# A decoder block in fp32 on one core: the short convolution's taps, moves, gating and high and low parts spread over steps of their own

## The chip, the core and the metric

The kernel runs on one core of a Trainium2 chip. The metric is the device time of one execution in microseconds. A core has five engines that work at the same time, each through its own instructions in order: TensorE (PE in the profile; its weight loads are PEld), VectorE (DVE), ScalarE (ACT), GpSimd (POOL) and SyncE (SP, which here only starts transfers). The program orders the instructions of TensorE, VectorE, ScalarE and GpSimd itself.

## The reference, cut to what matters

```python
hn = rmsnorm(x, g_mix)
proj = hn @ w_in                        # (512, 1024) x (1024, 14344)
xa, ba, ca, za, q, k, v, o, zb, ig, fg, ga, gb = split(proj)
u = ca * xa
y = up[0:s]*w[0] + up[1:s+1]*w[1] + up[2:s+2]*w[2] + b     # up: u with two zero rows in front
ya = (ba * y * silu(za)) @ w_a_out
yb = (...mLSTM over q, k, v with the gates i, f, o, zb...) @ w_b_out
merged = sigmoid(ga) * ya + sigmoid(gb) * yb
x = x + merged @ w_o
x = x + sigmoid(rmsnorm(x, g_ple) @ w_ple_gate) * (p @ w_ple)
out = rmsnorm(x, g_final)
```

All is float32; there are 512 positions and 1024 features.

## The kernel before, in words

**Products.** Every fp32 operand is cut into a high part (rounded to fp32r) and a low part (the rest), and a product is made of three matmuls: high x high, low x high, high x low (`mm3`, L234 to L236). The large products go through one level of Strassen's scheme: seven products of half the size in place of eight (`strassen`). Each of the seven is done in two halves (i = 0, 1) of 12 matmuls, so such a block has 14 half-products.

**Steps.** Behind each half-product the program calls `step`, which runs `tick`. A tick writes out, in this order: the first piece of the work that the half-product before handed over (`fresh`); one half of the next weight's cut (`split_half`: the high part `whi` on ScalarE, L181, the low part `wlo` on VectorE, L182, and where the scheme needs sums of weights an add on VectorE, L186, or accumulating DMAs from GpSimd's queue, L157); then one piece of every generator in `active`. Each `yield` in a generator ends its piece. So a yield moves what follows to the next half-product's place in the order of all four engines. The weight for the next product is cut while the present one runs, from one of four raw tiles (`wraw`); `whi` and `wlo` have two buffers for each half. In a conv block the raw tile of the first product is used again for the third, fifth and seventh, after the accumulating DMAs have added other weights to it.

**The convolution.** It goes over four blocks of 256 channels, c = 0, 2, 4, 6 (L1084 and L1085). `sink_conv` says what happens to the results of a block. `sink(0, t, src)` gets ca and xa for 128 positions t and puts their product u into a part of `m`; for t = 2 and 3 ScalarE first copies one factor from PSUM to a temporary `cx` (tag `e`, two buffers). `sink(1, ...)` makes ba * silu(za) from `zb` (L468 to L471) and, in all blocks but the last, turns it in 32x32 blocks (L474). `after()` then finishes the block during the next block's half-products (for c = 6, during the first product with `w_a_out`): TensorE turns u (`turned`, L403, eight transposes into `ptu`), ScalarE applies the tap of the current position with the bias (L426), VectorE adds the two earlier taps (`taps`, L409), ScalarE moves the 16 pieces of the turned gate into place (L445), VectorE multiplies by the gate (L412), ScalarE takes the high part into `ya` (L413) and VectorE the low part (`rest`, L416). In the last block the gate is turned on TensorE too, and there are no moves.

**Around it.** The convolution's buffer `m` first holds the output of head 3, which leaves for DRAM (`yt_d`) while the first block runs. Behind the convolution come the products with `w_a_out`, whose left operand is `ya`, then those with `w_b_out`, `w_o` and `w_ple_gate`.

Of the kernel before, what the change touches and what calls it, by code (L numbers as in the profile page):

```python
# [11 lines left out]
AF = mybir.ActivationFunctionType  # L12
ALU = mybir.AluOpType

P = 128
S = 512
NT = S // P
# [19 lines left out]
def hybrid_block(ctx, tc, x, p, g_mix, w_in, conv_w, conv_b, w_a_out, b_gates, g_head,  # L37
                 w_b_out, w_o, g_ple, w_ple_gate, w_ple, g_final, out):
    nc = tc.nc
    act, dve, pool, pe = nc.scalar, nc.vector, nc.gpsimd, nc.tensor  # L40
# [29 lines left out]
    H2 = S // 2  # L70
# [71 lines left out]
    raws, splits, pieces, active, fresh = {}, {}, deque(), [], []  # L142
# [60 lines left out]
    def next_operand(follow=True):  # L203

        i = state["use"]
        state["use"] += 1
        while pieces:
            split_half(*pieces.popleft())
        if follow:
            queue_split()  # L210
        got = splits.pop(i)
        return [[got[kt // HH][u][:, kt % HH, :] for kt in range(HC)] for u in range(2)]
# [71 lines left out]
    def temp(tag, name=None, dt=F32):  # L284

        return tp.tile([P, S], dt, name=name or tag, tag=tag, bufs={"c": 3}.get(tag, 2))
# [3 lines left out]
    def bank(m, tag=None):  # L290
        return ps_mm.tile([P, S], F32, name="mm", tag=tag or order[m // 2], bufs=2)
# [98 lines left out]
    def sink_conv(c, zb, ya, last):  # L390


        w = [[cw[:, j * KT + c + f:j * KT + c + f + 1] for j in range(3)] for f in range(2)]
        b = [cb[:, c + f:c + f + 1] for f in range(2)]
        u, blocks = (m[:, i, :].rearrange("p (t f) -> p t f", t=NT) for i in (2, 3))
        g, v = (m[:, i, :].rearrange("p (f s) -> p f s", f=2) for i in range(2))
        gs = [g[:, f, :] for f in range(2)]

        def turned(src):
            pts = [ps_x.tile([P, S], F32, name="ptu", tag="x") for _ in range(2)]  # L400
            for f in range(2):
                for t in range(NT):
                    pe.transpose(pts[f][:, t * P:(t + 1) * P], src[:, t, f * P:(f + 1) * P], ident)  # L403
            return pts

        def taps(f, pt):
            for j in (1, 0):
                to = v[:, f, 2 - j:]
                dve.scalar_tensor_tensor(to, pt[:, :S - 2 + j], w[f][j], to, ALU.mult, ALU.add)  # L409

        def gated(f):
            dve.tensor_tensor(v[:, f, :], v[:, f, :], gs[f], ALU.mult)  # L412
            act.activation(ya[0][:, c + f, :], v[:, f, :], AF.Copy)  # L413

        def rest(f):
            dve.tensor_tensor(ya[1][:, c + f, :], v[:, f, :], ya[0][:, c + f, :].bitcast(F32), ALU.subtract)  # L416

        def after():
            for _ in range(0 if last else 2 if c == 0 else 1):
                yield  # L420
            pts = turned(u)
            if last:
                gs[:] = turned(zb)
            yield
            for f in range(2):
                act.activation(v[:, f, :], pts[f], AF.Identity, scale=w[f][2], bias=b[f])  # L426
            yield
            if not ya:
                ya.extend(hp.tile([P, KT, S], F32R, name=f"ya{i}", tag=t, align_bytes=256) for i, t in enumerate(("qk", "vv")))
            if last:  # L430
                for f in range(2):
                    taps(f, pts[f])
                    gated(f)
                yield
                for f in range(2):
                    rest(f)
                return
            for i in range((P // B) ** 2):
                if i % 2 == 0:
                    if i < 4:  # L440
                        taps(i // 2, pts[i // 2])
                k, q = divmod(i, P // B)
                src = blocks[k * B:(k + 1) * B].rearrange("p t (f q a) -> p t f q a", q=P // B, a=B)[:, :, :, q]
                dst = g[q * B:(q + 1) * B].rearrange("p f (t b a) -> p t f b a", t=NT, a=B)[:, :, :, k]
                act.activation(dst, src, AF.Copy)  # L445
                if i % 2:
                    yield
            gated(0)
            yield
            rest(0)  # L450
            gated(1)
            yield
            rest(1)

        def sink(n, t, src):
            if n == 0:
                x = src[:, :H2]
                if t > 1:
                    x = temp("e", "cx")[:, :H2]
                    act.activation(x, src[:, :H2], AF.Copy)  # L460
                dve.tensor_tensor(u[:, t, :], x, src[:, H2:], ALU.mult)
                if t == NT - 1:
                    active.append(after())
                yield
            elif t % 2:
                bs, zs = (zb[:, t - 1:t + 1, i * H2:(i + 1) * H2] for i in range(2))
                z = temp("e", "cz").rearrange("p (t f) -> p t f", t=2)
                act.activation(z, zs, AF.Sigmoid)  # L468
                dve.tensor_tensor(bs, bs, zs, ALU.mult)
                yield  # L470
                dve.tensor_tensor(bs, bs, z, ALU.mult)  # L471
                if not last:
                    yield
                    dve.transpose(blocks[:, t - 1:t + 1, :], bs)  # L474
        return sink
# [71 lines left out]
    def turn_x(k, ts=range(NT), pt=None):  # L547
        if pt is None:
            pt = ps_x.tile([P, S], F32, name="pt", tag="x")
        for t in ts:  # L550
            pe.transpose(pt[:, t * P:(t + 1) * P], xin[:, t, k * P:(k + 1) * P], ident)
        return pt
# [22 lines left out]
    def high(q):  # L575
        hi, _, raw = quarters[q]
        act.activation(hi, raw, AF.Copy)
# [56 lines left out]
    pts = [turn_x(k, first, bank(k)) for k in range(HC)]  # L634
# [18 lines left out]
    for g in range(2):  # L653
        src = wg_raw[:, :, g * NH:(g + 1) * NH]
# [10 lines left out]
    w = splits.pop(1)  # L665
# [46 lines left out]
    B = nc.vector.STREAM_SQUARE_SIZE  # L712
    rows32 = sp.tile([B, 8, S], F32, name="rows", tag="xin")
    rows = rows32[:NH]
    turned = sp.tile([B, 14, P], F32, name="turned")
# [60 lines left out]
    w = next_operand()  # L776
# [293 lines left out]
    for h in range(NH):  # L1070
        y, tools = head(h, qks[h])
# [7 lines left out]
    ya = []  # L1079
# [3 lines left out]
    zb = cvp.tile([P, NT, S], F32, name="zb")  # L1083
    for c in range(0, KT, 2):  # L1084
        strassen(hn_lhs, sink_conv(c, zb, ya, c == KT - 2), place=lambda n, t: zb[:, t, :] if n else temp("c"))  # L1085
# [84 lines left out]
    todo = deque((n, t) for n, ts in ((0, (0, 1)), (1, range(NT)), (0, (2, 3))) for t in ts)  # L1170
# [203 lines left out]
    for left, banks, tag, row, n, op, last in (  # L1374
# [7 lines left out]
        w = next_operand()  # L1382
# [50 lines left out]
    w = {}  # L1433
# [60 lines left out]
    q = [slice(CW, CW + CW // 2), slice(CW + CW // 2, D)]  # L1494
# [25 lines left out]
    y = [temp(u, "y") for u in "sv"]  # L1520
# [27 lines left out]
```

## Time and profile before

| | us |
|---|---|
| median of three executions | 845.43 (843.02 to 845.84) |
| the profiled execution | 842.41 |
| its span, first to last instruction | 840.6 |
| TensorE's matmuls busy | 825.1 |
| VectorE busy | 675.7 |
| ScalarE busy | 557.0 |
| GpSimd busy | 210.3 |

The mean granted clock of TensorE is 0.997, and the DMA engines move 203 GB/s on average. The convolution's blocks run from about 468 to 619 us of the span.

How to read the lines that follow: a row of a time-ordered view gives the start, the time taken, the engine, the line of the kernel, the operation and the tiles (written tile, arrow, read tiles); in brackets stands how long the engine sat idle before it and what ended that. A row of the table of waits gives who waited for whom, the total in us, how often, and the longest. A row of the table by stretches gives for each engine the busy time and the number of instructions, then TensorE's granted clock, the busy share of the DMA engines and GB/s. A busy TensorE is not a TensorE at its peak, since matmuls overlap.

### The profile page before, as it was taken

What the parts mean: (1) busy time and instruction counts of PE and PEld (TensorE: products, weight loads), DVE (VectorE), ACT (ScalarE), POOL (GpSimd) and SP (SyncE); (2) the same over time, 40 slices, a digit from 0 to 9 for tenths busy, and PEclk for the clock granted to TensorE, in tenths of its full rate; (3) what the DMA queues carried; (4) which work ended last, traced back from release to release, by engine and by line L of the source; (5) the groups of instructions that cost most, each with busy time, mean ns of one, the idle gap of its engine ahead of it and who ended that gap; (6) DMA issues with size and microseconds to landing.
All of it is one profiled execution on the core that took longest, in us unless ns stands there. A gap on an engine that the chain in (4) does not pass through costs nothing.

```text
span 840.6 us, 10885 instructions
## 1 busy us (share of the span) xinstructions
PE 825.1 (98%) x3889; PEld 689.4 (82%) x3889; DVE 675.7 (80%) x910; ACT 557.0 (66%) x850; POOL 210.3 (25%) x212
## 2 busy tenths in 40 slices
PE   9999999999999999999999999999989999999996
PEld 8888888888899988888888887787868888888885
DVE  6688767998888777789888897788785679999576
ACT  6567665778755766577876587676757367857553
POOL 4203122213125211320312434242420122131031
PEclk9999999999999999999999999999999999999998
DMA  9749789769969897994996899897987698899502
GB/s 307 279 143 185 159 212 223 198 212 261 228 144 183 220 218 186 251 224 155 274 226 149 173 211 194 174 193 164 220 321 257 149 243 202 204 257 225 195 1 100
DMA packets 102942, 170.65 MB, mean 203 GB/s; under 512 B 5664, under 2 KB 47700, under 8 KB 102120
## 3 DMA queue, kind: packets, MB, share of 16 engines
q0 software_dynamic: 39136, 69.28, 43.4%
q1 hardware_dynamic: 59968, 94.64, 34.3%
q10 hardware_dynamic: 3784, 6.04, 2.3%
q8 instruction: 30, 0.49, 0.2%
q14 instruction: 24, 0.20, 0.1%
HBM read 153.16 MB, written 16.79 MB: 202 GB/s over the span
## 4 chain that ended last, share of the span: by engine, by line
PE 88%; DVE 4%; ACT 3%; DMA 2%; issue 1%; POOL 0%; POOLq 0%; ACTq 0%; SPq 0%; DVEq 0%
PE mm L235 26%; PE mm L236 26%; PE mm L234 26%; DVE wlo L182 2%; DMA wraw<-in_w_in 2%; ACT whi L181 1%; PE pv L234 1%; PE pv L236 1%; PE pv L235 1%; DMA yt_d<-m 1%; PE mm L595 1%; PE mmp L595 1%; PE sc L236 1%; PE sc L235 1%; PE sc L234 1%
## 5 line engine op out<-in xcount | busy, mean ns | idle before, releaser
L182 DVE TENSOR_TENSOR wlo<-wraw,whi 128x1024 fp32r<-128x1024 f32 x245 | 300.5, 1228 | 82.8 <-ACT whi L181 76.2
L181 ACT ACTIVATE whi<-wraw 128x1024 fp32r<-128x1024 f32 x246 | 258.2, 1055 | 63.5 <-PE mm L236 40.9
L157 POOL DMA_DIRECT2D wraw<-in_w_in x106 | 129.4, 1467 | 297.4 <-DVE wlo L182 238.7
L235 PE MATMUL mm<-wlo,hs 128*128 128x512 f32 x384 | 149.7, 390 | 0.5 <-DVE wlo L182 0.5
L234 PE MATMUL mm<-whi,hs 128*128 128x512 f32 x384 | 149.6, 389 | 0.0
L236 PE MATMUL mm<-whi,hs 128*128 128x512 f32 x384 | 149.5, 389 | 0.0
L235 PE MATMUL mm<-wlo,hn_hi 128*128 128x512 f32 x288 | 112.6, 391 | 2.7 <-DVE wlo L182 2.7
L234 PE MATMUL mm<-whi,hn_hi 128*128 128x512 f32 x288 | 112.8, 392 | 0.9 <-ACT whi L181 0.9
L236 PE MATMUL mm<-whi,hn_lo 128*128 128x512 f32 x288 | 112.2, 389 | 0.0
L347 ACT ACTIVATE s<-mm 128x512 f32<-128x512 f32 x84 | 50.0, 596 | 61.5 <-PE mm L236 60.1
L235 PEld LDWEIGHTS mm<-wlo,hs 128*128 128x128 f32 x384 | 72.1, 188 | 15.6 <-DVE wlo L182 0.9
L236 PEld LDWEIGHTS mm<-whi,hs 128*128 128x128 f32 x384 | 72.1, 188 | 15.1
L234 PEld LDWEIGHTS mm<-whi,hs 128*128 128x128 f32 x384 | 72.1, 188 | 15.0 <-ACT whi L181 0.4
L235 PEld LDWEIGHTS mm<-wlo,hn_hi 128*128 128x128 f32 x288 | 54.1, 188 | 15.1 <-DVE wlo L182 4.1
L234 PEld LDWEIGHTS mm<-whi,hn_hi 128*128 128x128 f32 x288 | 54.1, 188 | 13.2 <-ACT whi L181 1.7
L236 PEld LDWEIGHTS mm<-whi,hn_lo 128*128 128x128 f32 x288 | 54.1, 188 | 11.2
L351 DVE TENSOR_TENSOR c<-s,mm 128x512 f32<-128x512 f32 x48 | 32.9, 684 | 16.3 <-ACT s L347 9.4
L234 PE MATMUL mm<-whi,l 128*128 128x512 f32 x112 | 43.8, 391 | 0.0
L235 PE MATMUL mm<-wlo,l 128*128 128x512 f32 x112 | 43.7, 390 | 0.0
L236 PE MATMUL mm<-whi,l 128*128 128x512 f32 x112 | 43.6, 389 | 0.0
L234 PE MATMUL mm<-hn_hi,whi 128*128 128x512 f32 (+1 forms) x112 | 39.0, 348 | 0.0
L235 PE MATMUL mm<-hn_lo,whi 128*128 128x512 f32 (+1 forms) x112 | 38.5, 344 | 0.0
(345 smaller groups left out, 1531.6 us busy)
## 6 DMA issues: line engine op xcount, KB each, us to landing
wraw<-in_w_in SPq DMA_DIRECT2D x32, 1024.0 KB, 5.8
wraw<-in_w_in SPq DMA_DIRECT2D x46, 512.0 KB, 4.9
wraw<-in_w_in POOLq DMA_DIRECT2D x46, 512.0 KB, 7.5
wraw<-in_w_in POOLq DMA_DIRECT2D x60, 256.0 KB, 5.9
wraw<-in_w_b_out SPq DMA_DIRECT2D x7, 1024.0 KB, 6.9
wraw<-in_w_b_out POOLq DMA_DIRECT2D x12, 512.0 KB, 7.2
wraw<-in_w_o SPq DMA_DIRECT2D x5, 1024.0 KB, 7.5
wraw<-in_w_a_out SPq DMA_DIRECT2D x4, 1024.0 KB, 6.0
```

Source lines behind the costliest of these rows:

```text
L157: nc.gpsimd.dma_start(raws[to][:, ks, cs], src[:, ks, :], accum_op=ALU.add)
L181: act.activation(hi, t, AF.Copy)
L182: (e_lo or dve).tensor_tensor(lo, t, hi.bitcast(F32), ALU.subtract)
L234: pe.matmul(ps, lhsT=a[0], rhs=b[0], start=first, stop=False, **kw)
L235: pe.matmul(ps, lhsT=a[0], rhs=b[1], start=False, stop=False, **kw)
L236: pe.matmul(ps, lhsT=a[1], rhs=b[0], start=False, stop=last, **kw)
L347: act.activation(to[i], src, AF.Copy, scale=scale)
L351: dve.tensor_tensor(c, u, v, op)
L595: pe.matmul(pss[n, t], lhsT=pT[u][:, k, t * P:(t + 1) * P], rhs=(whi, wlo)[v][2 * n + k], start=(k, i) == (0, 0), stop=(k, i) == (1, 2))
```

## The change

It is confined to `sink_conv`. Gating and high part become two functions and stand in steps of their own. The product u for t = 2 and 3 moves from `sink` into a generator of its own (`product_of`), so that it comes behind the weight cut of its step. `after()` goes by a plan that says for each step which first taps, how many of the 16 moves and which later taps it issues; the first block (`late`) has its own plan, which starts two steps later behind the transposes, while its transposes come one step earlier. In the last block the gate is turned one step later than u.

```diff
         def gated(f):
             dve.tensor_tensor(v[:, f, :], v[:, f, :], gs[f], ALU.mult)
+
+        def high(f):
             act.activation(ya[0][:, c + f, :], v[:, f, :], AF.Copy)
...
+        def first_tap(f, pt):
+            act.activation(v[:, f, :], pt, AF.Identity, scale=w[f][2], bias=b[f])
+
         def after():
-            for _ in range(0 if last else 2 if c == 0 else 1):
+            if not last:
                 yield
             pts = turned(u)
-            if last:
-                gs[:] = turned(zb)
-            yield
-            for f in range(2):
-                act.activation(v[:, f, :], pts[f], AF.Identity, scale=w[f][2], bias=b[f])
-            yield
-            if not ya:
+            yield
+            late = not ya
+            if late:
                 ya.extend(hp.tile([P, KT, S], F32R, name=f"ya{i}", tag=t, align_bytes=256) for i, t in enumerate(("qk", "vv")))
             if last:
                 for f in range(2):
+                    first_tap(f, pts[f])
+                gs[:] = turned(zb)
+                for f in range(2):
                     taps(f, pts[f])
+                yield
+                for f in range(2):
                     gated(f)
+                    high(f)
                 yield
                 for f in range(2):
                     rest(f)
                 return
-            for i in range((P // B) ** 2):
-                if i % 2 == 0:
-                    if i < 4:
-                        taps(i // 2, pts[i // 2])
...
-                act.activation(dst, src, AF.Copy)
-                if i % 2:
-                    yield
-            gated(0)
-            yield
+            todo = deque(range((P // B) ** 2))
+            if late:
+                yield
+                yield
+                plan = (([0, 1], 0, []), ([], 3, []), ([], 3, [0]), ([], 4, [1]), ([], 4, []), ([], 2, []))
+            else:
+                plan = (([0], 1, []), ([1], 2, []), ([], 4, []), ([], 3, []), ([], 3, [0]), ([], 3, [1]))
+            for firsts, n, others in plan:
+                for f in firsts:
+                    first_tap(f, pts[f])
+                for f in others:
+                    taps(f, pts[f])
+                for _ in range(n):
+                    move(todo.popleft())
+                yield
+            assert not todo
+            for some in (gated, high):
+                for f in range(2):
+                    some(f)
+                yield
             rest(0)
-            gated(1)
             yield
             rest(1)
+
+        def product_of(t, x, y):
+            dve.tensor_tensor(u[:, t, :], x, y, ALU.mult)
+            if t == NT - 1:
+                active.append(after())
+            yield
 
         def sink(n, t, src):
             if n == 0:
-                x = src[:, :H2]
-                if t > 1:
-                    x = temp("e", "cx")[:, :H2]
-                    act.activation(x, src[:, :H2], AF.Copy)
-                dve.tensor_tensor(u[:, t, :], x, src[:, H2:], ALU.mult)
-                if t == NT - 1:
-                    active.append(after())
+                if t < 2:
+                    dve.tensor_tensor(u[:, t, :], src[:, :H2], src[:, H2:], ALU.mult)
+                    return
+                x = temp("e", "cx")[:, :H2]
+                act.activation(x, src[:, :H2], AF.Copy)
+                active.append(product_of(t, x, src[:, H2:]))
                 yield
```

(`move(i)` holds the four lines that were in the loop over the 16 moves.)

What the change does to the order of instructions is shown at two places. The first is VectorE at the end of the last block (c = 6) and the start of the products with `w_a_out`. `wlo` are weight cuts, one to a step; `m<-cx,mm` is the product u for t = 2 and then t = 3; `zb` is the gate. Before:

```order
L461 TENSOR_TENSOR m<-cx,mm 128x256
L182 TENSOR_TENSOR wlo_5549<-wraw_5269,whi_5548 128x1024
L416 TENSOR_TENSOR ya_4674<-m,ya_4673 128x512
L469 TENSOR_TENSOR zb<-zb 128x2x256
L461 TENSOR_TENSOR m<-cx,mm 128x256
L182 TENSOR_TENSOR wlo_5600<-wraw_5375,whi_5599 128x1024
L471 TENSOR_TENSOR zb<-zb,cz 128x2x256
L182 TENSOR_TENSOR wlo_5638<-wraw_5375,whi_5637 128x1024
```

And now, at the same place (L494 and L496 are what L469 and L471 were, L476 is the product):

```order
L182 TENSOR_TENSOR wlo_5549<-wraw_5269,whi_5548 128x1024
L494 TENSOR_TENSOR zb<-zb 128x2x256
L476 TENSOR_TENSOR m<-cx,mm 128x256
L182 TENSOR_TENSOR wlo_5599<-wraw_5374,whi_5598 128x1024
L496 TENSOR_TENSOR zb<-zb,cz 128x2x256
L476 TENSOR_TENSOR m<-cx,mm 128x256
L182 TENSOR_TENSOR wlo_5628<-wraw_5374,whi_5627 128x1024
```

Each product has moved from the front of its step, ahead of `wlo`, to its end; the low part of the block before (L416) has left this step.

The second is ScalarE over the last steps of the same block and the first of the next stage. `s` are results taken out of PSUM, `whi` weight cuts, `ya` high parts, `cz` a sigmoid for the gate, `cx` the copied factor. Before:

```order
L413 ACTIVATE ya_4673<-m 128x512
L468 ACTIVATE cz<-zb 128x512
L347 ACTIVATE s<-mm 128x512
L181 ACTIVATE whi_5525<-wraw_5269 128x1024
L413 ACTIVATE ya_4673<-m 128x512
L460 ACTIVATE cx<-mm 128x256
L181 ACTIVATE whi_5548<-wraw_5269 128x1024
L468 ACTIVATE cz<-zb 128x512
L460 ACTIVATE cx<-mm 128x256
L181 ACTIVATE whi_5599<-wraw_5375 128x1024
```

And now:

```order
L415 ACTIVATE ya_4630<-m 128x512 x2
L347 ACTIVATE s<-mm 128x512
L181 ACTIVATE whi_5484<-wraw_4933 128x1024
L347 ACTIVATE s<-mm 128x512
L181 ACTIVATE whi_5504<-wraw_4933 128x1024
L493 ACTIVATE cz<-zb 128x512
L347 ACTIVATE s<-mm 128x512
L181 ACTIVATE whi_5529<-wraw_5269 128x1024
L487 ACTIVATE cx<-mm 128x256
L181 ACTIVATE whi_5548<-wraw_5269 128x1024
L493 ACTIVATE cz<-zb 128x512
L487 ACTIVATE cx<-mm 128x256
```

The two high parts stand together and two steps earlier than the first of them stood, and between a `whi` and the `cx` ahead of it nothing is left that VectorE's gating must release.

On TensorE the eight transposes of u in the first block stand one half-product earlier, and those of the gate in the last block one half-product later; on SyncE's queue one load of `sga` has moved ahead of one of `w_a_out`. GpSimd's order is the same.

More of the change, by code (lines that the diff above doesn't have):

```diff
@@ L416, in rest, with move @@
             dve.tensor_tensor(ya[1][:, c + f, :], v[:, f, :], ya[0][:, c + f, :].bitcast(F32), ALU.subtract)
+        def move(i):
+            k, q = divmod(i, P // B)
+            src = blocks[k * B:(k + 1) * B].rearrange("p t (f q a) -> p t f q a", q=P // B, a=B)[:, :, :, q]
+            dst = g[q * B:(q + 1) * B].rearrange("p f (t b a) -> p t f b a", t=NT, a=B)[:, :, :, k]
+            act.activation(dst, src, AF.Copy)
+        def first_tap(f, pt):
+            act.activation(v[:, f, :], pt, AF.Identity, scale=w[f][2], bias=b[f])
         def after():
-            for _ in range(0 if last else 2 if c == 0 else 1):
+            if not last:
                 yield
             pts = turned(u)
-            if last:
-                gs[:] = turned(zb)
             yield
-            for f in range(2):
-                act.activation(v[:, f, :], pts[f], AF.Identity, scale=w[f][2], bias=b[f])
-            yield
-            if not ya:
+            late = not ya
+            if late:
                 ya.extend(hp.tile([P, KT, S], F32R, name=f"ya{i}", tag=t, align_bytes=256) for i, t in enumerate(("qk", "vv")))
@@ L437, in after @@
                 return
-            for i in range((P // B) ** 2):
-                if i % 2 == 0:
-                    if i < 4:
-                        taps(i // 2, pts[i // 2])
-                k, q = divmod(i, P // B)
-                src = blocks[k * B:(k + 1) * B].rearrange("p t (f q a) -> p t f q a", q=P // B, a=B)[:, :, :, q]
-                dst = g[q * B:(q + 1) * B].rearrange("p f (t b a) -> p t f b a", t=NT, a=B)[:, :, :, k]
-                act.activation(dst, src, AF.Copy)
-                if i % 2:
-                    yield
-            gated(0)
-            yield
+            todo = deque(range((P // B) ** 2))
[18 more added lines that the diff above has]
+                yield
             rest(0)
-            gated(1)
             yield
             rest(1)
+        def product_of(t, x, y):
[3 more added lines that the diff above has]
+            yield
         def sink(n, t, src):
             if n == 0:
-                x = src[:, :H2]
-                if t > 1:
-                    x = temp("e", "cx")[:, :H2]
-                    act.activation(x, src[:, :H2], AF.Copy)
-                dve.tensor_tensor(u[:, t, :], x, src[:, H2:], ALU.mult)
-                if t == NT - 1:
-                    active.append(after())
+                if t < 2:
[4 more added lines that the diff above has]
+                active.append(product_of(t, x, src[:, H2:]))
                 yield
```

## The prediction

> **What bounds the kernel now.** I read the busy times first, then who waited for whom on TensorE, then the stretches around the convolution, then the order of time at the waits.
>
> ```profile
> PE 825.1 (98%) x3889; PEld 689.4 (82%) x3889; DVE 675.7 (80%) x910; ACT 557.0 (66%) x850; POOL 210.3 (25%) x212
> PE mm L235 <- DVE wlo L182: 3.9, 6, 0.8
> PE mm L234 <- ACT whi L181: 1.8, 2, 0.9
> PE ptu L403 <- DVE zb L471: 0.8, 1, 0.8
> 470.00:510.00 40.00, 40.00 (x182) 33.20 (x181) 32.90 (x43) 28.58 (x39) 18.33 (x16) 1.00 0.98 210
> 510.00:550.00 40.00, 37.57 (x165) 29.67 (x164) 32.57 (x40) 29.41 (x48) 11.55 (x10) 1.00 0.84 173
> 550.00:590.00 40.00, 38.33 (x171) 31.01 (x171) 31.85 (x40) 28.49 (x46) 14.25 (x13) 1.00 0.89 183
> 590.00:630.00 40.00, 37.57 (x172) 30.35 (x171) 32.69 (x40) 26.49 (x42) 12.77 (x15) 1.00 0.94 265
> ```
>
> The kernel is bound by TensorE, and TensorE's waits inside the program lie in the convolution: 2.43 + 1.67 + 2.43 = 6.53 us of idle time from 510 to 630 us, in 6 + 2 + 1 = 9 waits. In all but one the releaser is a weight tile that is cut too late (`whi` by ScalarE, `wlo` by VectorE). Both engines have room (VectorE 32.6 of 40 us), so the waits come from when things are done, not from how much there is to do.
>
> ```profile
> 507.39 0.39 PE L234 MATMUL mm<-whi,hs 128*128 128x512 f32 x1
> 514.19 0.39 PE L234 MATMUL mm<-whi,hs 128*128 128x512 f32 x1
> 515.08 0.50 PE L235 MATMUL mm<-wlo,hs 128*128 128x512 f32 x1 [0.51 <-DVE wlo L182]
> 515.42 0.40 PE L236 MATMUL mm<-whi,hs 128*128 128x512 f32 x1
> ```
>
> What a wait costs is more than its idle time. Thirty matmuls start between 507.39 and 514.19, 0.227 us apart, so half a product (12 matmuls) takes 2.72 us. Around the wait the starts are 0.89 and 0.34 us apart: 0.66 + 0.11 = 0.77 us lost where the row counts 0.51. I add that 0.26 to each of the nine: 6.53 + 9 x 0.26 = **8.9 us** are lost, and this is the most the change can win. [...]
>
> ```profile
> 576.86 0.68 DVE L416 TENSOR_TENSOR ya<-m,ya 128x512 fp32r<-128x512 f32 x1
> 577.46 0.68 DVE L412 TENSOR_TENSOR m<-m 128x512 f32<-128x512 f32 x1
> 578.17 0.63 ACT L413 ACTIVATE ya<-m 128x512 fp32r<-128x512 f32 x1 [2.50 <-DVE m L412]
> 578.71 0.37 ACT L460 ACTIVATE cx<-mm 128x256 f32<-128x256 f32 x1
> 578.98 1.05 ACT L181 ACTIVATE whi<-wraw 128x1024 fp32r<-128x1024 f32 x1
> 580.05 1.23 DVE L182 TENSOR_TENSOR wlo<-wraw,whi 128x1024 fp32r<-128x1024 f32 x1 [0.52 <-ACT whi L181]
> 580.08 0.50 PE L234 MATMUL mm<-whi,hn_hi 128*128 128x512 f32 x1 [0.92 <-ACT whi L181]
> 581.20 0.68 DVE L416 TENSOR_TENSOR ya<-m,ya 128x512 fp32r<-128x512 f32 x1
> 581.34 0.50 PE L235 MATMUL mm<-wlo,hn_hi 128*128 128x512 f32 x1 [0.76 <-DVE wlo L182]
> ACT ya L413 <- DVE m L412: 18.0, 8, 3.3
> ```
>
> This is the end of the third block (c = 4). ScalarE's `ya` (L413) stands still 2.50 us for VectorE's gating of the same step (L412); behind it in ScalarE's queue stand `cx` and `whi`, behind `whi` VectorE's `wlo`, and TensorE waits twice. The same happens near 538 and 621 us. Of ScalarE's idle time before L413, 18.0 us in 8 times come from L412.
>
> **The change part by part.** *Gating and high parts in steps of their own.* In a block that isn't the last, both gatings now stand after the split of one step, both high parts after the split of the next. At 2.72 us a step, VectorE has finished two gatings (0.60 apart, 577.46 to 578.06) before ScalarE gets to L415, and behind L415 no weight is late. This takes away what led to the waits near 538, 546, 579, 581, 621 and 622. Nothing is added: the same two gatings, high parts and low parts are issued.
>
> *Taps and moves later, and the late plan of the first block.*
>
> ```profile
> 507.32 1.45 ACT L426 ACTIVATE m<-ptu,prm 128x512 f32<-128x512 f32 x2 [2.65 <-DMA yt_d<-m]
> 508.66 1.06 ACT L181 ACTIVATE whi<-wraw 128x1024 fp32r<-128x1024 f32 x1
> 517.86 3.49 DVE L182 TENSOR_TENSOR wlo<-wraw,whi 128x1024 fp32r<-128x1024 f32 x3
> 519.37 4.90 POOL L157 DMA_DIRECT2D wraw<-in_w_in  x4 [10.07 <-DVE wlo L182]
> 529.97 1.06 ACT L181 ACTIVATE whi<-wraw 128x1024 fp32r<-128x1024 f32 x1 [1.26 <-DMA wraw<-in_w_in]
> ```
>
> Behind the first block the first taps (L426) block ScalarE 2.65 us until head 3's copy of `m` has left for `yt_d`; `whi` follows 1.3 us later, VectorE then does adds and taps ahead of three `wlo` (517.86), and the wait at 515.08 results. The late `wlo` also holds back POOL's four accumulating DMAs (519.37); their data comes at 529.97, which gives the wait near 532. In the new order the first taps stand one step (2.7 us) and one `whi` later, when the copy is nearly out; taps move to the steps in which VectorE has no add and no L351. So these two go as well. The transposes of this block come one step earlier on TensorE; they are the same eight.
>
> *The product for t = 2 and 3 behind the split.* Here something is added. Before, `m<-cx` (L461) ran ahead of the `wlo` of its step; now (L476) it runs last in the step. ScalarE's `cx` for t = 3 writes the buffer of `cx` for t = 2 (tag `e` has two), so it waits for L476 of t = 2, and `whi` is queued behind it. The transposes of `u` on TensorE wait for L476 of t = 3, and all later matmuls stand behind them.
>
> ```profile
> 582.42 0.65 DVE L469 TENSOR_TENSOR zb<-zb 128x512 f32<-128x512 f32 x1
> 583.00 0.41 DVE L461 TENSOR_TENSOR m<-cx,mm 128x256 f32<-128x256 f32 x1
> 583.33 1.21 DVE L182 TENSOR_TENSOR wlo<-wraw,whi 128x1024 fp32r<-128x1024 f32 x1
> 584.46 0.68 DVE L471 TENSOR_TENSOR zb<-zb,cz 128x512 f32<-128x512 f32 x1
> 585.06 1.22 DVE L182 TENSOR_TENSOR wlo<-wraw,whi 128x1024 fp32r<-128x1024 f32 x1
> 581.80 0.70 DVE L474 STREAM_TRANSPOSE m<-zb 128x512 f32<-128x512 f32 x1
> L830 DVE COPY m<-yc x6: 417/420/425, 485.0 to 499.4; 32x512 f32<-32x512 f32 x6
> 626.03 0.88 PE L403 MATMUL ptu<-ident,zb 128*128 128x128 f32 x6 [0.75 <-DVE zb L471]
> 626.66 0.48 PE L234 MATMUL mm<-whi,ya 128*128 128x512 f32 x1
> ```
>
> The chain in the last block, counted from the end of its 13th half-product, by spacings in the rows: `cx` to `whi` 0.27, `whi` to `wlo` 1.07, `wlo` to the next 1.15 (580.05 to 581.20), L469 0.58, product 0.41: 3.48 us. Then `cx` for t = 3: 0.27 + 1.07 + 1.13, L471 0.60, product 0.41: 3.48 again. The product stands at 6.96 us. TensorE gets there after two half-products, 5.44 us: a new wait of **1.5 us** (1.75 if each hand-over takes some 0.03 us more), which with 0.26 for the restart makes 1.9. It takes the place of the wait at 626.03 (0.75 + 0.26), which goes, because the transposes of `zb` now come a step later. In the other three blocks `u` is transposed one half-product later, at 8.16 us, and the step has extra work: L474 with 0.62 (581.80 to 582.42) gives 7.6 in the third; in the second a low part of the first block (0.60, 576.86 to 577.46) makes it 8.2, in the first two of head 3's moves (L830, 0.42 each) make it 8.4. So one block has 0.6 us to spare, one just meets the time and one is 0.3 us late; with its restart that is 0.55. New waits in all: 1.9 + 0.55 = **2.45 us**. Their bounds: nothing, if VectorE gets ahead, and some 4 us, if all four boundaries wait like the last.
>
> *The rest.* SyncE issues one load of `sga` ahead of a `w_a_out` load that is used some 20 us later, at no cost. POOL's order is unchanged; its adding DMAs follow the `wlo`, which come earlier or on time.
>
> **The sum.** 8.9 lost now, 2.45 lost after: 6.5 us less. The profiled execution took 842.41 us (span 840.6, and 1.8 around it), so 835.9. It is the fastest seen; the median of the three runs is 845.43, 3.0 above it, so for the median I forecast **838.9 us** (-0.8%). About 0.3% (2.5 us) is what a measurement of this kernel can tell from no change.
>
> [...]
>
> **The rivals.**
> 1. *Nothing new in place of the nine waits.* VectorE reaches the products early enough. 845.43 - 8.9 = 836.5. Against it: 6.96 against 5.44 us in the last block. Chance 0.10.
> 2. *Part of it goes: the adding DMAs stay late.* From a `wlo` to the next cut of the same raw tile there are four half-products, 10.9 us; from the end of the second of the three `wlo` (517.86 + 1.14 + 1.22 = 520.2) to the data at 529.97 it took 9.75. With DMA engines busy 0.84 to 0.94 of the time, and less time to do it in, three or four such waits of 0.6 + 0.26 could stay: 838.9 + 3.5 = 842.4. Chance 0.13.
> 3. *No change:* the recurring gap is a matter of buffers, or later stages give the time back, since the loads for `w_b_out` and `yf` fall into 590 to 630 us, the stretch with the most traffic (265 GB/s). Against the second: after 630 us no wait of TensorE is in the table, and those loads are released by the same steps. 845.4, within 0.3%. Chance 0.11.
> 4. *Slower: the adding DMAs are late in every block.* Each product that reuses a raw tile (three per block, two halves, three blocks with taps: 18 cuts) would wait as at 529.97, 0.86 each: 18 x 0.86 = 15.5, and 15.5 + 2.45 - 8.9 = +9, 854 us. It decides once `wlo` slips against `whi` by more than 10.9 - 9.75 = 1.1 us; 11 such waits would already undo the gain. For it: each tap pair (1.5 us) sits right in the steps in which these tiles are cut. Against it: the taps stand behind that step's `wlo`, not ahead of it. Chance 0.05.
>
> **How the numbers follow.** The forecast has 0.61, the rivals 0.10, 0.13, 0.11 and 0.05. Faster by over 0.3%: 0.61 + 0.10 + most of rival 2 (0.11) = 0.82; within 0.3%: 0.11 + 0.02 = 0.13; slower 0.05. For the range, the lower end is rival 1 with half the distance of the median to the fastest run (836.5 - 1.5 = 835.0); the upper end is rival 2, 843.0 with its rounding. Rivals 3 and 4 lie outside, 0.16 together.
>
> **What would show it.** Right: no rows of idle time before the high parts (L415) by L412; no TensorE wait for `whi` or `wlo` between 510 and 630 us; one row for `ptu` waiting 1.5 to 1.8 us for the product (L476) after the first half-product of the `w_a_out` stage, and TensorE's idle time from 510 to 630 us down from 6.5 to about 2. Wrong: rows `whi` <- DMA with more than a few tenths, a wait for `ptu` at all four boundaries, or a TensorE wait after 630 us that was not there. If the waits are gone and the time is the same, the 0.26 per wait or the stage behind is what I misjudged.

## The result and the profile after

The changed kernel takes **835.78 us** in the median (835.72 to 837.03, five executions) against 845.09 (843.02 to 845.84, five executions) for the kernel before: a ratio of 0.9897 with a 95% interval of 0.9882 to 0.9912. The profiled execution took 835.72 us, its span is 833.9; before it was 842.41 and 840.6. The profiled executions are thus 6.7 us apart and the medians 9.3.

The engines' busy times on the page after, then the rows of the table of waits that concern the change (who waits for whom, us in total, times, longest), TensorE's first:

```profile
PE 821.6 (99%) x3889; PEld 689.0 (83%) x3889; DVE 674.4 (81%) x910; ACT 556.8 (67%) x850; POOL 210.5 (25%) x212
PE ptu L403 <- DVE m L476: 2.1, 2, 1.5
ACT cx L487 <- DVE m L476: 8.3, 4, 2.7
ACT ya L415 <- DVE m L412: 3.0, 1, 3.0
ACT m L427 <- DMA yt_d<-m: 0.2, 1, 0.2
```

VectorE and ScalarE do the same work as before (674.4 against 675.7 us, 556.8 against 557.0). In the convolution the rows for `wlo` and `whi` (6 + 2 waits) and the one for `zb` are gone, and one new row stands in their place: the transposes of u (`ptu`) wait for the product (L476). Outside it the table has 0.9 us for a `whi` of another product (L602), 6 us into the program, where the change does nothing; in the other profiles this wait lies between nothing and 0.8 us. ScalarE's idle time before the high part by the gating has gone from 18.0 us in 8 times to 3.0 in one, in the last block, where gating and high part still stand in turn.

The same four stretches as before (busy us of PE, PEld, DVE, ACT, POOL, then clock, DMA share, GB/s):

```profile
470.00:510.00 40.00, 39.39 (x178) 32.51 (x177) 33.52 (x44) 28.43 (x38) 18.21 (x16) 1.00 0.96 204
510.00:550.00 40.00, 39.94 (x181) 32.95 (x180) 33.59 (x42) 32.03 (x53) 15.07 (x13) 1.00 0.96 198
550.00:590.00 40.00, 40.00 (x182) 33.23 (x181) 33.88 (x42) 29.64 (x47) 14.74 (x13) 1.00 0.93 192
590.00:630.00 40.00, 38.52 (x179) 31.87 (x178) 32.09 (x41) 25.89 (x39) 9.19 (x12) 1.00 0.95 295
```

From 510 to 630 us TensorE now stands idle 0.06 + 0 + 1.48 = 1.54 us, where it was 6.53. A further 0.61 us has appeared ahead of 510, behind the first block.

The end of the last block in order of time (start, time taken, engine, line, operation, tiles; in brackets the idle time before it and what ended it):

```profile
611.35 0.38 ACT L487 ACTIVATE cx<-mm 128x256 f32<-128x256 f32 x1 [1.11 <-PE mm L236]
611.63 1.05 ACT L181 ACTIVATE whi<-wraw 128x1024 fp32r<-128x1024 f32 x1
612.72 1.23 DVE L182 TENSOR_TENSOR wlo<-wraw,whi 128x1024 fp32r<-128x1024 f32 x1 [0.46 <-ACT whi L181]
614.46 0.41 DVE L476 TENSOR_TENSOR m<-cx,mm 128x256 f32<-128x256 f32 x1
614.99 0.39 ACT L487 ACTIVATE cx<-mm 128x256 f32<-128x256 f32 x1 [1.79 <-DVE m L476]
615.27 2.00 ACT L181 ACTIVATE whi<-wraw 128x1024 fp32r<-128x1024 f32 x2
616.36 1.23 DVE L182 TENSOR_TENSOR wlo<-wraw,whi 128x1024 fp32r<-128x1024 f32 x1 [1.48 <-ACT whi L181]
618.10 0.41 DVE L476 TENSOR_TENSOR m<-cx,mm 128x256 f32<-128x256 f32 x1
618.57 0.76 PE L403 MATMUL ptu<-ident,m 128*128 128x128 f32 x5 [1.48 <-DVE m L476]
```

This is the chain of the prediction, link by link: `cx`, `whi`, `wlo`, product; then `cx` for t = 3, which ScalarE holds 1.79 us for that product because it needs its buffer; then `whi`, `wlo`, product again; and TensorE, 1.48 us late. No weight is late any more in this place.

### The profile page after: what moved, and what is told of

Its sections match the earlier page's. It is cut to its first block, busy times and chain, and to the rows that moved or that the text cites. A ratio compares the mean times of both kernels' runs of the same rounds, so it can differ in the third digit from the quotient of the medians.

```text
span 833.9 us, 10890 instructions
## 1 busy us (share of the span) xinstructions
PE 821.6 (99%) x3889; PEld 689.0 (83%) x3889; DVE 674.4 (81%) x910; ACT 556.8 (67%) x850; POOL 210.5 (25%) x212
## 4 chain that ended last, share of the span: by engine, by line
PE 92%; DVE 3%; ACT 2%; DMA 2%; issue 1%; POOLq 0%; ACTq 0%; POOL 0%; DVEq 0%
PE mm L234 28%; PE mm L235 28%; PE mm L236 28%; DMA xin<-in_x 1%; PE pv L236 1%; PE pv L235 1%; PE pv L234 1%; PE sc L236 1%; PE sc L235 1%; PE sc L234 1%; ACT whi L181 1%; PE ptu L403 0%; DVE wlo L182 0%; DMA pin<-in_p 0%; PE ptk L1358 0%
## 5 line engine op out<-in xcount | busy, mean ns | idle before, releaser
L234 PE MATMUL mm<-whi,hs 128*128 128x512 f32 x384 | 149.6, 390 | 0.0
L234 PE MATMUL mm<-whi,hn_hi 128*128 128x512 f32 x288 | 112.3, 390 | 0.0
L347 ACT ACTIVATE s<-mm 128x512 f32<-128x512 f32 x84 | 50.1, 597 | 62.1 <-PE mm L236 60.5
L234 PEld LDWEIGHTS mm<-whi,hs 128*128 128x128 f32 x384 | 72.1, 188 | 15.0 <-ACT whi L181 0.4
L234 PEld LDWEIGHTS mm<-whi,hn_hi 128*128 128x128 f32 x288 | 54.1, 188 | 11.0
L234 PE MATMUL mm<-whi,l 128*128 128x512 f32 x112 | 43.8, 391 | 0.0
L234 PE MATMUL mm<-hn_hi,whi 128*128 128x512 f32 (+1 forms) x112 | 39.0, 348 | 0.0
L236 PE MATMUL mm<-hn_hi,wlo 128*128 128x512 f32 (+1 forms) x112 | 38.5, 344 | 0.0
```

Source lines behind the costliest of these rows:

```text
L234: pe.matmul(ps, lhsT=a[0], rhs=b[0], start=first, stop=False, **kw)
L236: pe.matmul(ps, lhsT=a[1], rhs=b[0], start=False, stop=last, **kw)
L347: act.activation(to[i], src, AF.Copy, scale=scale)
```

## The experiments

**Once more, both kernels.** The changed kernel and the kernel before, run again.

> The changed kernel once more, so that its variants can be compared on one chip. Both theories: 835.7 to 837, TensorE waiting for the product in the first and in the last block, about 0.6 and 1.5 us.

> The kernel before once more, with a second profile. Its median was 845.1 in five runs but 842.4 in the profiled one. Theory (the waits for weights lie close to the time at which adding transfers land, so they vary from run to run): nine waits again, but of other sizes, and if this execution is slower than 842.4 by 1 us or more, its TensorE waits between 510 and 630 us are larger by as much. Rival (the time around the span, or another stage, varies): the nine waits are within 0.3 us of the first profile whatever the time.

Measured: 836.01 us (835.56 to 836.69) for the changed kernel, a ratio of 0.9903 (0.9885 to 0.9920); 843.81 (842.75 to 845.58, ten executions) for the copy of the kernel before, against 844.0 for the original, a ratio of 0.9998 (0.9988 to 1.0009). The gain repeats, 8.0 us. The changed kernel's two new waits are 0.62 and 1.47 us here, as expected. The kernel before spreads over 3 us from one execution to the next and the changed one over 1. My theory of that spread failed: the profile of the kernel before is 1.9 us longer than its first one (842.5 against 840.6), yet TensorE's idle time from 510 to 630 us is smaller, 5.92 against 6.53. The rival didn't hold in full either. Six of the nine waits have their old lengths; the two behind the first block have changed from 0.51 and 0.59 to 1.03 and 0.12, and the one for `zb` is gone. And the profile has something that the first one didn't have: a lower clock.

The transposes behind the last two weight waits, on TensorE, in that execution of the kernel before:

```profile
622.68 0.50 PE L234 MATMUL mm<-whi,ya 128*128 128x512 f32 x1 [0.92 <-ACT whi L181]
623.94 0.50 PE L235 MATMUL mm<-wlo,ya 128*128 128x512 f32 x1 [0.76 <-DVE wlo L182]
...
625.24 1.91 PE L403 MATMUL ptu<-ident,m 128*128 128x128 f32 x8
626.94 1.85 PE L403 MATMUL ptu<-ident,zb 128*128 128x128 f32 x8
628.51 0.51 PE L234 MATMUL mm<-whi,ya 128*128 128x512 f32 x1
```

And TensorE's stretches at that place (busy us, then the granted clock of TensorE, DMA share, GB/s):

```profile
624.00:626.00 2.00, 2.00 (x9) 0.80 1.01 418
626.00:628.00 2.00, 2.00 (x11) 0.50 1.00 415
628.00:630.00 2.00, 2.00 (x11) 0.85 1.01 416
```

The granted clock falls to 0.50 here for (0.20 + 0.50 + 0.15) x 2 / 0.5 = 3.4 us, and eight transposes take 1.70 us (625.24 to 626.94) instead of the 0.88 below. I come back to it under the last experiment.

**The product back in front of the cut, the rest as changed.**

```diff
                 act.activation(x, src[:, :H2], AF.Copy)
-                active.append(product_of(t, x, src[:, H2:]))
+                dve.tensor_tensor(u[:, t, :], x, src[:, H2:], ALU.mult)
+                if t == NT - 1:
+                    active.append(after())
                 yield
```

> The product of t = 2 and 3 stands ahead of the weight cut again, all else as changed. Theory (the product behind the cut is a cost of its own: 0.6 + 1.5 us of waits and 0.3 near 542, with 0.26 for each restart): TensorE no longer waits for the product, 2.5 to 3 us less than the changed kernel, 833. Rival (the move of the product is needed for the gain, since VectorE then waits for cx ahead of wlo): waits for wlo come back at the block ends, and the time is 836 to 840.

Measured: **832.84 us** (832.79 to 833.10), a ratio of 0.9865 (0.9848 to 0.9882), as the theory had it. It beats both kernels and hardly spreads. TensorE in the four stretches of its profile:

```profile
470.00:510.00 40.00, 40.00 (x183) 1.00 0.98 211
510.00:550.00 40.00, 40.00 (x182) 1.00 0.97 196
550.00:590.00 40.00, 40.00 (x183) 1.00 0.93 194
590.00:630.00 40.00, 40.00 (x186) 1.00 0.95 297
```

Nothing waits in the convolution. The product's move, one of the parts of the change, is therefore a loss of 3.2 us (836.01 - 832.84), and the other parts are worth more than the change as a whole: 11.2 us (844.0 - 832.84).

**Another buffer for the second `cx`.** The order stays as changed; `cx` for t = 3 no longer writes the buffer of `cx` for t = 2 (between the two the sigmoid `cz` takes the other buffer of tag `e`). Is the new wait a matter of the buffer or of the order?

```diff
-                x = temp("e", "cx")[:, :H2]
+                x = temp("e" if t == 2 else "v", "cx")[:, :H2]
```

> The copy cx for t = 3 goes to a buffer of another tag (v, free at that time), so that it does not wait for the product of t = 2; the order of all instructions stays. Theory (the new wait is half buffer, half order): the chain to the last product falls from 6.96 to 2.72 + 0.27 + 1.07 + 1.13 + 0.60 + 0.41 = 6.20 us against 5.44, so the wait in the last block falls from 1.5 to about 0.75 and that in the first block goes; 1.4 to 1.9 us less, 834.2. Rival (it is the order alone, VectorE gets to the product no earlier): both waits stay within 0.2 us and the time within 0.3 us of the changed kernel.

Measured: 834.36 us (833.67 to 835.75), a ratio of 0.9885 (0.9862 to 0.9908). TensorE's row for the product in the table of waits:

```profile
PE ptu L403 <- DVE m L476: 0.6, 1, 0.6
```

The wait of the first block is gone and that of the last has shrunk from 1.48 to 0.56 us. So 0.9 us of the latter come from the buffer, the rest from the product's place behind the cut. A third buffer under the tag `e` was not tried.

**Gating and high parts in steps of their own, nothing else.** The kernel before with this one part of the change. This experiment and the next three ran on another chip, where the kernel before takes 844.19 us (844.0 on the chip of those above).

```diff
+        def high(f):
             act.activation(ya[0][:, c + f, :], v[:, f, :], AF.Copy)
...
-            gated(0)
-            yield
+            for some in (gated, high):
+                for f in range(2):
+                    some(f)
+                yield
             rest(0)
-            gated(1)
             yield
             rest(1)
```

> The kernel before with one part of the change alone: gating and high parts in steps of their own in the blocks that are not the last; taps, moves and products stand as before. Theory (six of the nine waits come from ScalarE's high part waiting in turn for the gating ahead of a weight that is due): the waits near 538, 546, 580, 581, 621 and 622 go, 4.7 + 6 x 0.26 = 6.3 us in the profile, and the two of the first block and that for the gate's transposes stay: span 834 to 836. With no two waits close together the executions lie within 1.5 us of each other, and TensorE's clock stays at 1.00 from 30 to 800 us. Rival (the gain needs taps and moves in their new steps): waits stay at the block ends, 839 or more.

Measured: 837.84 us (836.83 to 839.82), a ratio of 0.9921 (0.9903 to 0.9940). TensorE's waits in the convolution, as its rows in the table of waits:

```profile
PE mm L235 <- DVE wlo L182: 2.0, 2, 1.6
PE mm L236 <- DVE l L1111: 1.2, 1, 1.2
PE ptu L403 <- DVE zb L475: 0.5, 1, 0.5
```

The waits for `whi` and `wlo` at the ends of the blocks are gone but for 0.49 us at 539.15, which is most of the gain of 6.3 us. I had expected a span of 834 to 836 and a narrower spread. The span is 836.3: the wait behind the first block (516.24) has grown from 0.51 to 1.55, and in this execution a wait of 1.2 us stands outside the convolution. The executions spread over 3 us although the clock of this profile is not halved anywhere before the program's end, so the halved clock is not the whole of the spread. The wait near 516 needs the first block's part of the change, which comes next.

**The late plan of the first block, nothing else.** The kernel before, with the first block's transposes one step earlier, its first taps three steps behind them in place of one, later taps, and 3, 3, 4, 4 and 2 moves to a step (the lines for taps and moves are left out here).

```diff
-            for _ in range(0 if last else 2 if c == 0 else 1):
+            for _ in range(0 if last else 1):
                 yield
             pts = turned(u)
...
+            late = not ya
+            if late:
+                yield
+                yield
             for f in range(2):
                 act.activation(v[:, f, :], pts[f], AF.Identity, scale=w[f][2], bias=b[f])
```

> The kernel before with the first block's new plan alone (transposes one step earlier, first taps one step later, taps and moves as changed); gating in turn as before. Theory: the two waits near 515 and 532 go, 1.6 us in the profile, the six at the block ends stay. These come in pairs of 0.92 and 0.76 us, 1.3 us apart, and in some executions such a pair halves TensorE's clock for 3.4 us as in the second profile of the kernel before; so the executions stay spread over 2 us or more, about 842.5 in the median. Rival for the spread (late adding transfers of the first block): without the first two waits the spread falls under 1.5 us.

Measured: 843.47 us (841.82 to 847.00), a ratio of 0.9987 (0.9974 to 1.0000): by itself this part is worth next to nothing. The wait near 515 is gone and that near 532 is down to 0.14 us, but a new one stands where the first block's results are gated. The profile is that of the slowest execution, 847.0. ScalarE and TensorE there:

```profile
534.32 0.63 ACT L413 ACTIVATE ya<-m 128x512 fp32r<-128x512 f32 x1 [2.49 <-DVE m L412]
534.86 0.61 ACT L474 ACTIVATE cz<-zb 128x512 f32<-128x512 f32 x1
535.38 0.58 ACT L347 ACTIVATE s<-mm 128x512 f32<-128x512 f32 x1
536.00 0.51 PE L234 MATMUL mm<-whi,hn_hi 128*128 128x512 f32 x1 [1.44 <-ACT s L347]
```

ScalarE stands 2.49 us for VectorE's gating; behind it in the queue is the copy `s` (L347) that takes a half-product's result out of PSUM, the buffer into which TensorE writes; TensorE waits 1.44 us for that copy. The stall takes another victim, not a weight. The spread stays at 5 us, so the first block's two waits were not its cause.

**Gating in turn again, but early.** The changed kernel with gating and high part of each half in one step and its low part in the next, right behind the last taps, where I thought that no weight is due.

```diff
-            for some in (gated, high):
-                for f in range(2):
-                    some(f)
+            for f in range(2):
+                gated(f)
+                high(f)
                 yield
-            rest(0)
-            yield
-            rest(1)
+                rest(f)
```

> The changed kernel with gating and high part again in one step and in turn, but in the steps right behind the taps, three earlier than in the kernel before. Theory (a wait in turn costs only where a weight that is due stands behind it): ScalarE waits for the gating again, 1 to 3 us each time, but no weight is late, and the time is that of the changed kernel within 0.6 us. Rival (waiting in turn costs by itself): the waits for whi and wlo come back, 839 or more.

Measured: 842.44 us (842.16 to 844.24), a ratio of 0.9981 (0.9970 to 0.9992). My theory that waiting in turn is harmless where no weight is due has fallen. TensorE's rows in the table of waits, then ScalarE and TensorE where the third block's results are gated:

```profile
PE mm L234 <- ACT s L347: 3.3, 3, 1.4
PE ptu L403 <- DVE m L474: 2.7, 3, 1.5
```

```profile
610.83 0.63 ACT L415 ACTIVATE ya<-m 128x512 fp32r<-128x512 f32 x1 [2.49 <-DVE m L412]
611.36 0.58 ACT L347 ACTIVATE s<-mm 128x512 f32<-128x512 f32 x1
...
612.00 0.50 PE L234 MATMUL mm<-whi,hs 128*128 128x512 f32 x1 [0.92 <-ACT s L347]
```

It is the mechanism of the experiment above, once for each of the first three blocks (1.42, 0.92 and 0.92 us): ScalarE's queue holds up whatever stands behind the high part, be it `whi` or the copy out of PSUM. My rival had the time right (839 or more) and the victim wrong, since the waits for `whi` and `wlo` stay away but for 0.14 us. Gating and high part in turn cost 6.4 us here (842.44 - 836.01, on two chips), as much as taking them apart gained in the kernel before (6.3).

**Gating in turn, at the steps of the kernel before.** The changed kernel, with gating and high part in turn and three steps (two in the first block) put ahead of them.

```diff
-            for some in (gated, high):
-                for f in range(2):
-                    some(f)
+            for _ in range(2 if late else 3):
                 yield
-            rest(0)
-            yield
-            rest(1)
+            for f in range(2):
+                gated(f)
+                high(f)
+                yield
+                rest(f)
```

> The changed kernel with gating and high part in one step, in turn, and in the same steps as in the kernel before (at the end of the next block). Theory: the waits at the block ends come back, near 540, 580 and 620 us, 4.7 us of idle time and 6.3 lost, and the new wait for the product stays: about 841 to 843, with a spread of 2 us or more as waits stand close together. Rival (the taps and moves in their new steps leave enough room): within 1.5 us of the changed kernel.

Measured: 850.04 us (849.02 to 850.96), a ratio of 1.0064 (1.0047 to 1.0081): slower than the kernel before. I had said slower than the changed kernel, which is right, but missed the size by 7 us. TensorE's rows in the table of waits, the last block's chain, and three stretches with the clock:

```profile
PE ptu L403 <- DVE m L476: 6.3, 3, 3.3
PE mm L234 <- ACT whi L181: 1.8, 2, 0.9
PE mm L235 <- DVE wlo L182: 1.5, 2, 0.8
```

```profile
621.93 0.63 ACT L415 ACTIVATE ya<-m 128x512 fp32r<-128x512 f32 x1 [2.50 <-DVE m L412]
622.47 0.37 ACT L487 ACTIVATE cx<-mm 128x256 f32<-128x256 f32 x1
...
626.16 0.41 DVE L476 TENSOR_TENSOR m<-cx,mm 128x256 f32<-128x256 f32 x1
626.69 0.38 ACT L487 ACTIVATE cx<-mm 128x256 f32<-128x256 f32 x1 [2.39 <-DVE m L476]
...
630.26 1.24 PE L403 MATMUL ptu<-ident,m 128*128 128x128 f32 x5 [3.31 <-DVE m L476]
```

```profile
545.00:549.00 4.00, 4.00 (x12) 0.57 0.78 243
582.00:586.00 4.00, 3.76 (x10) 0.58 0.88 116
630.00:634.00 4.00, 3.74 (x12) 0.57 1.02 422
```

Four weight waits came back, near 581 and 624 us; those that I had expected near 540 did not. Two things add to them. The late `cx` now pushes the product behind the cut too, so that its wait grows from 1.48 to 3.31 us in the last block, and the second block has one of 2.42. And the clock is halved three times, for 3.4 us each. Matmuls then start 0.427 us apart in place of 0.227 (four steps from 631.72 to 633.43), so that eight of them fit into the 3.4 us and some 1.6 us are lost a time. Together, as an estimate: 6.3 - 2.1 = 4.2 for the product, 1.8 + 1.5 for the weights with 4 x 0.26 for their restarts, and 4.8 for the clock, 13.3 us in all; from 468 us on the two kernels are 13.8 apart (379.2 - 365.4).

**The kernel before, three more profiles.** Why is its profiled execution 842.41 and its median 844 to 845?

> The kernel before, one profiled execution. My theory of the spread: an execution takes the 840.6 us of the first profiled one plus 1.7 to 1.9 us for each stretch of 3.41 us in which the granted clock falls to 0.50 close behind the waits of the convolution (between 510 and 640 us); with none of them the span is 840 to 841.5 us, with one 842 to 843, with two 844 to 845, and TensorE's waits in that stage stay 6 to 7.5 us in all. Rival: the executions differ in the waits' own lengths; then the span moves by the change of the waits' sum, and the clock does not tell the executions apart.

> The same kernel once more, with the same expectation: span = 840.6 us + 1.7 to 1.9 us for each stretch of 3.41 us at a clock of 0.50, within 0.7 us; by the rival it follows the sum of TensorE's waits instead.

> The same kernel a third time, with the same expectation: span = 840.6 us + 1.7 to 1.9 us for each stretch of 3.41 us at a clock of 0.50, within 0.7 us; by the rival it follows the sum of TensorE's waits instead.

Measured, with the kernel before's two other profiles and the changed kernel's. The third column is the start of the first matmul on the sums `hs` in the convolution (L234, `mm<-whi,hs`), the fourth the rest of the span, and the fifth runs from the matmul behind the last `wlo` wait to the first matmul behind the transposes that follow:

| execution | span | first matmul on `hs` | rest of the span | wait to matmul behind the transposes | clock halved |
|---|---|---|---|---|---|
| before, first | 840.6 | 468.28 | 372.3 | 622.76 to 626.66: 3.90 | no |
| before, second | 842.5 | 469.06 | 373.4 | 623.94 to 628.51: 4.57 | once |
| before, third | 843.2 | 469.08 | 374.1 | 624.66 to 629.18: 4.52 | once |
| before, fourth | 842.0 | 469.29 | 372.7 | 624.17 to 628.07: 3.90 | no |
| before, fifth | 840.8 | 468.55 | 372.3 | 622.94 to 626.84: 3.90 | no |
| changed, first | 833.9 | 468.50 | 365.4 | | no |
| changed, second | 833.9 | 468.44 | 365.5 | | no |

(The first block itself begins at 457.2 us, four half-products ahead of that matmul, and not at 468 as I put it above; nothing in those four differs between the kernels.)

My theory holds in part only. The fifth profile fits it. The fourth is a miss: no halved clock and 842.0, where I had put it under 841.5; it got to the convolution 1.0 us later than the first profile, which neither theory had. The third, with one halved clock, is 843.2, where I had put it at 843 at most. And a halved clock costs this kernel 0.65 us net, not 1.7, since it takes up the wait for the gate's transposes. The same place at full clock, in the fifth profile:

```profile
624.21 1.04 PE L403 MATMUL ptu<-ident,m 128*128 128x128 f32 x8
625.09 0.38 PE L403 MATMUL ptu<-ident,zb 128*128 128x128 f32 x2
626.21 0.87 PE L403 MATMUL ptu<-ident,zb 128*128 128x128 f32 x6 [0.74 <-DVE zb L471]
```

The transposes are quicker by 0.8 us and TensorE then waits 0.74 us for `zb`; at half clock it arrives when `zb` is done. The rival, that the waits' own lengths differ, has its share: the third profile has another wait of 0.53 us, at 600.36, and the waits for `wlo` sum to 4.6 us instead of 3.9. So the 2.6 us between these five profiles have three small causes: the start (up to 1.0 us), the clock (0.65) and the waits (up to 0.7 more, in the third).

The executions without a profile spread further, up to a span of 846.0. For 46 executions on two chips the record has the mean granted clock beside the span: those at 0.997 or 0.998 have a mean span of 841.7 us (17 executions, 840.6 to 843.4), those at 0.994 or 0.995 one of 842.8 (14 executions, 841.2 to 846.0). The clock thus goes with about 1 us, and spans at like clocks differ by 3 us and more, so the larger part of the spread isn't explained.

## Why the prediction was right

**The nine waits.** All went. Six of them are the mechanism of the prediction, high parts that held up ScalarE's queue in front of `whi`: taking gating and high parts apart, by itself, leaves 0.49 of these 4.7 us, and putting them back in turn at the old steps brings four of the six back. The two behind the first block went by its late plan, which takes 0.51 to nothing and 0.59 to 0.14 us by itself, and the one for `zb` as the gate's transposes come a step later. In the kernel with the product in front nothing of the nine is left and nothing new has come, so its rest of the span gives their price: 372.3 us before, 362.6 there (831.0 - 468.42). That is 9.7 us; I had put the most there is to win at 8.9. Counted matmul by matmul, all of it arises in the convolution and the first steps of the products with `w_a_out`; from 632 us to the end the two kernels drift apart by no more than 0.03 us. The idle rows hold 6.53 of it, so that a wait costs about 0.35 more than its row, where I had 0.26 from one of them.

**The new waits.** Forecast were 1.5 to 1.75 us in the last block, 0.3 in the first, "just meets" in the second and 0.6 to spare in the third. Measured: 1.48 and 0.61 us; in the second block the transposes are followed by a spacing of 1.07 us, where the third has the usual 0.79, so some 0.28; in the third nothing. With restarts I had 2.45 us; the rest of the span is 365.4 against 362.6 without these waits, so 2.8.

**The sum.** 6.5 us were forecast for the profiled execution, 6.7 were measured. That it comes so close is in part luck: what was to be won was 0.8 us too small, the new waits 0.35 too small, and the changed kernel's profile got to the convolution 0.2 us later.

**The rivals.** Rivals 2 and 4 needed adding DMAs that stay late. In the convolution no row of TensorE waiting for `whi` or `wlo` is left; the taps' wait for the copy to `yt_d` went from 2.7 to 0.2 us. Rival 3's doubt on buffers is answered by the two experiments on the product: the buffer is 0.9 us of the new wait, and none of the nine, which go without any new buffer. Rival 1 had no new waits, and 2.1 us of them are there. By the time alone one couldn't tell: 835.78 lies nearer to that rival's 836.5 than to the forecast.

**The step that was mis-sized** is the one from the profile to the median. The forecast for the median was 838.9, 3.1 us more than the 835.78 measured, which lies only 0.8 above the lower end of the range. I added to 835.9 the 3.0 us by which the first median had stood above the profiled execution, as if they would stay. The changed kernel's median stands 0.1 us above its profile. The five executions of the kernel before in the table show where the difference comes from: the mean rest of the span is 373.0, 0.7 above the first profile's (halved clock and extra small waits, which go with the nine waits), and the mean start is 468.85, 0.6 above. The halved clocks and the small waits belong to what the change takes away; the start doesn't, since it is 469.23 in the kernel with the other buffer too. These means account for 1.2 of the 3.0 us. The rest stays open: an execution without a profile shows only its span and its mean clock, and the clock goes with about 1 us of the spread.

**What was forecast or read wrongly beside it.** I said that no idle time before a high part by the gating would be left; 3.0 us are, in the last block. No TensorE wait hangs on it. The wait at 515.08 does not come from the three `wlo` at 517.86, which start later: its `wlo` runs at 513.81, behind an add (510.90), the taps (512.03) and a product (513.48). And under rival 4, eight waits of 0.86 us would have undone the gain of 6.45, not eleven.

## What to carry to other kernels

Where two engines hand work to and fro and one of them also serves TensorE, do all of one engine's half in one step and the other's in a later one: what a stalled instruction costs is decided by what is queued behind it, here a weight's cut (TensorE waited 0.92 and 0.76 us), and, when that was out of the way, the copy that takes a result out of PSUM (0.92 to 1.44 us). A change made of several moves should be taken apart even when it wins: one of these moves cost 3.2 of the 11.2 us that the others won. And when a median is forecast from a profiled execution, what lies between the two may belong to the very waits that the change removes.

## What the runs showed of the hardware

**A halved clock came behind waits of 0.92 and 0.76 us, and behind one of 1.44, in some executions.** In the kernel before, two waits of 0.92 and 0.76 us, 1.26 us from start to start, stand near 581 and again near 623 us. Those near 623 were followed in two of five profiles by 3.4 us at a granted clock of 0.50; in the other three, and near 581 in all five, they weren't. One wait of 1.44 us was followed by it in the kernel with the first block's plan alone (the first row), which had it a second time further on, behind a pair of waits near 583:

```profile
536.00:540.00 4.00, 4.00 (x11) 0.57 0.43 148
584.00:588.00 4.00, 4.00 (x13) 0.57 0.94 121
```

The changed kernel's wait of 1.48 us had none in both its profiles, nor had the one of 1.42 us in the kernel with gating in turn but early (mean clock 0.998). Seven such stretches stand in these traces, the program's last microseconds aside. Those that the rows place begin 1.3 us after the wait of 0.76 us in the second profile of the kernel before (625.2 against 623.94), 0.4 us after the one of 1.44 (536.4 against 536.00) and within 0.2 us after the one of 3.31 in the kernel with gating in turn at the old steps; the kernel without waits in the convolution has none, at 1.00 from 470 to 630 us. That the waits cause them is the likely reading, and no run separates it from others. Where the tables of stretches here and under the experiments show one, it lasts 3.4 us. Why the same waits were followed by one in some executions only is not shown.

**What a halved clock costs depends on what comes next.** It was 0.65 us where TensorE would have waited 0.74 us anyway, and it is some 1.6 where nothing takes it up, by the spacing of the matmuls in the kernel with gating in turn at the old steps.
